# Hybrid decoder layer on one core: GpSimd's clears and copies moved or delayed, gate weights over its own queue, half of the value pages gathered, decay load and decay factors ahead

## The chip, the core and the metric

The kernel runs on one core of a Trainium2 chip. The metric is the device time of one execution in microseconds, the median of several runs; lower is better. The engines are named as in the profile: PE (TensorE), DVE (VectorE), ACT (ScalarE), POOL (GpSimd) and SP (SyncE, which here only issues transfers). POOL too issues transfers, plain ones and gathers by a list of row numbers.

## The reference

One step of a decoder layer for a prompt of 512 tokens and, beside it, 8 sample sequences of 4 new tokens each (544 token columns in all, model width 1024). The mixer has 8 attention heads of a native sparse attention (NSA: a compressed, a selected and a window branch, 2 key/value heads of 64) and 4 heads of gated linear attention (GLA: keys of 64, values of 128, chunks of 32 tokens). The parts that the change touches, in float32:

```python
def gla_branch(q_g, k_g, v_g, lr, w_gk, b_gk, s0):
    log_a = jax.nn.log_sigmoid((lr @ w_gk + b_gk)) / GLA_NORMALIZER
    o, S = gla_chunked(q_g, k_g, v_g, log_a.reshape(B, T, GLA_HEADS, GLA_DK), s0)
...
def mixer_output(o_cmp, o_slc, o_win, gates, o_gla, g_gla, gla_norm, w_o):
    o_nsa = gates[:, :, 0] * o_cmp + gates[:, :, 1] * o_slc + gates[:, :, 2] * o_win
    o_g = rmsnorm(o_gla, gla_norm) * jax.nn.silu(g_gla)
    return jnp.concatenate([o_nsa, o_g], axis=-1) @ w_o
...
past = cache_kv[page_table].reshape(B, past_len, 4, NSA_KV_HEADS, HEAD_DIM)
```

Here `lr` (16 columns), `g_gla` (512 columns), the queries, keys and values are all column groups of one projection of the normed input. Past keys and values of the samples lie in pages of 128 rows, 8 pages for each of the 8 sequences, in an order that a page table gives. After the mixer come a SwiGLU layer (inner width 2816), a gated per-layer embedding and a last norm.

## The kernel before, in words

Activations are kept feature by token: 8 slices of 128 features by 544 columns, in two halves of 256 and 288 columns. Every projection runs in three matmuls on split numbers: a value x is xh (rounded to the matmul's type) plus xl (the rest), a weight is `wh` plus `wl`, and `acc3` (L140) adds wh·xh, wh·xl and wl·xh. `fetch` (L115) loads 128 × 1024 weights (512 KB) over SP's queue into one of two `wraw` buffers; `load_w` (L122) makes `wh` from it, on ACT or (with `lo=POOL`) on POOL at L130, and `wl` by a subtraction, on DVE at L137 in one piece or on POOL at L135 in four pieces of 256 columns. `fm_tile` loads one such tile and runs its 2 × 24 matmuls into `pj`.

The instructions of each engine run in order. The order comes from a scheduler that goes by the order of the program, by data, and by hints: `issue_after` puts an instruction behind a given one, `together` (L46) draws a group of matmuls ahead and ties it to the loads that it needs.

The mixer goes through these places, with their times in the profiled execution:

- **Compression and queries, up to 136 us.** `compress_pages` gathers pages and compresses blocks of keys and values (`cps`); beside it `gates` (L515), the query tiles `q0` to `q3`, and behind the last compressed block `decays` (L534 to L561). It loads the small weight `wgk`, clears `w3` and `g3` (named `w` and `g` in the trace) on POOL, fills them with the split halves of `wgk` and of `glr` on ACT and DVE (L542 to L547), and multiplies them on PE (`zps`). The logarithm of the decay, `ls`, goes to memory (`lsd`) over POOL's queue.
- **Attention, 136 to 272 us**, prompt blocks and sample scores, with key pages loaded by SP beside it.
- **The GLA stretch, from 272 us.** The tile `gg0` of the GLA gate projection runs on PE. Small constants and `ls` are loaded (L997 to L1008). For the samples, `sps` sums the decays, ACT and DVE make `qs`, `ksm` and `kds`, POOL copies `qs` into `qm` (L1029), cleared before (L1016), and `oiq` multiplies `qm` by the old states. For the prompt, `gla_front` (L1048) makes `bps` and `rps`, and fills `kdz`, which POOL cleared (L1046). `gla_states`, `gla_out` and `gla_gate` follow.
- **The values of the samples, 278 to 373 us.** `s_values` (L943) is a generator: `tick` takes four steps of it behind each half of a gate tile. A step is one of 13 key tiles `kt` of a group `bg` of four sequences: tiles 0 to 7 are cache pages, 8 to 11 window rows, the last is new tokens. A page tile takes four pages into one of four `vch` buffers. One of its four pages is gathered by POOL (`gather_page`, L97), the other three are loaded by SP (`load_page`, L101), which first reads the page's number into a register.
- **Output projection, from about 375 us.** The first products (`pk`) of `wo` start while the last values and gate tiles end, and then the rest of the layer, up to 908 us.

The three hints that set the work around the change are:

```python
ready.append((load_page if b4 else gather_page)(vt[:, b4, :], m, i["pgv"]))
...
with tc.issue_after(pe[0].ins), together(ready, 5 * AHEAD):
...
def tile_gg(j, lo=POOL):
    fm_tile(f"gg{j}", ev_silu(j), lo=lo, then=tick)
```

Of the kernel before, what the change touches and what calls it, by code (L numbers as in the profile page):

```python
# [9 lines left out]
F32 = mybir.dt.float32  # L10
F32R = mybir.dt.float32r
# [10 lines left out]
TT = SEQ + NS  # L22
# [9 lines left out]
FM = FM_GLA + FM_NSA  # L32
# [3 lines left out]
def kernel(ctx: ExitStack, tc: tile.TileContext, i: dict, o: dict):  # L36
# [4 lines left out]
    def pool(name, bufs=1, space=None, stack=ctx, side=None):  # L41
        kw = {"reuse_waits": "tile"}
        if space is not None:
            kw["space"] = space
        if side is not None:
            kw["side"] = side  # L46
        return stack.enter_context(tc.tile_pool(name=name, bufs=bufs, **kw))
# [64 lines left out]

    third, count = [], [0, 0, 0]

    def fetch(src, n):  # L115
        own, b = (third[0], 1) if third and count[1] % 3 == 0 else (wp, 2)
        raw = own.tile([128, 1024], F32, name="wraw", bufs=b)
        count[1] += 1
        sp[0] = SP.dma_start(raw[:, :n], src)
        return raw  # L120

    def load_w(src, n, lo=None, dst=None, raw=None):  # L122
# [408 lines left out]
            DVE.tensor_copy(gate[bg], ps[:, 0:4])  # L531


    def decays(dp):  # L534

        wgk = dp.tile([64, 256], F32, name="wgk")
        SP.dma_start(wgk[32:49, :], i["wgk"])
        w3 = dp.tile([96, 256], F32R, name="w3")
        g3 = dp.tile([96, TT], F32R, name="g3")
        for t in (w3, g3):  # L540
            POOL.memset(t.bitcast(F32), 0.0)
        ACT.copy(w3[32:49, :], wgk[32:49, :])  # L542
        ACT.copy(w3[64:81, :], wgk[32:49, :])
        DVE.tensor_sub(w3[0:17, :], wgk[32:49, :], w3[32:49, :])
        ACT.copy(g3[32:49, :], glr[32:49, :])
        ACT.copy(g3[0:17, :], glr[32:49, :])
        DVE.tensor_sub(g3[64:81, :], glr[32:49, :], g3[32:49, :])  # L547
        ls = dp.tile([128, 5, 256], F32, name="ls")
        zm = dp.tile([128, 5, 256], F32, name="zm")
        POOL.memset(ls[:, 4, :], 0.0)  # L550
        POOL.memset(zm[:, 4, :], 0.0)
        for a, b, n in ((0, 2, 128), (2, 4, 128), (4, 5, 32)):
            ps = g1("zps").rearrange("p (t c) -> p t c", t=2)
            for t in range(a, b):
                mm(ps[:n, t - a, :], g3[:, 128 * t:128 * t + n], w3)
            ACT.activation(ls[:n, a:b, :], ps[:n, 0:b - a, :], AF.Abs)
            ACT.activation(zm[:n, a:b, :], ps[:n, 0:b - a, :], AF.Relu, scale=-1.0)
            ACT.activation(ls[:n, a:b, :], ls[:n, a:b, :], AF.Exp, scale=-1.0)
        ACT.activation(ls, ls, AF.Ln, bias=1.0)
        POOL.tensor_tensor(ls, zm, ls, op=ALU.add)  # L560
        POOL.dma_start(lsd, ls)  # L561
# [63 lines left out]
    later[3][1]()  # L625
    compress_prompt()
    gates()

    SP.dma_start(rowv, i["rowv"])
    rv = tp_.tile([128, 2496], F32, name="rv")  # L630
# [19 lines left out]
    first.close()  # L650
    y = compress_pages()
    with ExitStack() as dcy:
        decays(pool("dp", stack=dcy))
    fm_tile("q3", ev_q(3))
    second_layer(y)
    cpool.close()
# [274 lines left out]
    gp = pool("gp", stack=nsa)  # L931
# [11 lines left out]
    def s_values():  # L943
        for bg in range(2):
            P = SG[bg][0]
            O = psg.tile([128, 512], F32, name="sO", tag="sO", bufs=1)
            for kg_ in range(4):
                n = min(4, 13 - 4 * kg_)
                tp = proj_ps("sT")
                pT = sp_.tile([128, 512], F32, name="pT", bufs=2)  # L950
                for j in range(n):
                    kt = 4 * kg_ + j
                    w = 128 if kt < 12 else 72
                    PE.transpose(tp[0:w, 128 * j:128 * j + 128], P[:, 128 * kt:128 * kt + w], ident)
                if n == 4:
                    (ACT.copy if kg_ % 2 else DVE.tensor_copy)(pT, tp)
                else:
                    DVE.tensor_copy(pT[0:72, 0:128], tp[0:72, 0:128])
                for j in range(n):
                    kt = 4 * kg_ + j  # L960
                    w = 128
                    ready = []
                    if kt < 8:
                        vt = sp_.tile([128, 4, 128], F32, name="vch", bufs=4)
                        for b4 in range(4):
                            m = 8 * (4 * bg + b4) + kt
                            ready.append((load_page if b4 else gather_page)(vt[:, b4, :], m, i["pgv"]))
                    elif kt < 12:
                        vt = sp_.tile([128, 4, 128], F32, name="vch", bufs=4)
                        ready.append(SP.dma_start(vt, i["winv"][bg, kt - 8]))  # L970
                    else:
                        vt, w = VT[:, 4 * bg:4 * bg + 4, :], 72
                    with tc.issue_after(pe[0].ins), together(ready, 5 * AHEAD):
                        for b4 in range(4):
                            c = 128 * j + 32 * b4
                            mm(O[32 * b4:32 * b4 + 32, 0:128], pT[0:w, c:c + 32], vt[0:w, b4, :], start=kt == 0, stop=kt == 12)
                    yield
            Os = sp_.tile([128, 128], F32, name="Os", bufs=2)
            ACT.copy(Os, O[:, 0:128])
            tp = g1("sOT")  # L980
            PE.transpose(tp[:, 0:128], Os, ident)
            for g in range(2):
                DVE.tensor_copy(om_n[64 * g:64 * g + 64, :, SEQ + 16 * bg:SEQ + 16 * bg + 16].rearrange("p r (b t) -> p b r t", t=4),
                                tp[64 * g:64 * g + 64, 0:128].rearrange("p (b h r t) -> p b h r t", b=4, h=2, r=4)[:, :, g])
# [6 lines left out]
            next(values, None)  # L991

    def tile_gg(j, lo=POOL):
        fm_tile(f"gg{j}", ev_silu(j), lo=lo, then=tick)


    tri = gp.tile([128, 3, 128], F32, name="tri")  # L997
    SP.dma_start(tri, i["tri"])
    tri4 = gp.tile([32, 3, 32], F32, name="tri4")
# [4 lines left out]
    SP.dma_start(glan, i["glan"])  # L1004
    glah = gp.tile([128, 1], F32, name="glah")
    DVE.tensor_scalar_mul(glah, glan, 0.5)
    ls = gp.tile([128, 5, 256], F32, name="ls")
    SP.dma_start(ls, lsd)  # L1008


    qs = gp.tile([128, 2, NS], F32, name="qs")
# [1 line left out]
    ksm = gp.tile([128, 2, NS], F32, name="ksm")  # L1013
    kds = gp.tile([128, 2, NS], F32, name="kds")
    Es = gp.tile([128, 2, NS], F32, name="Es")
    POOL.memset(qm, 0.0)  # L1016
    for ip in range(2):
        cs = slice(ip * 128, ip * 128 + 128)
        sps = g1("sps")
# [6 lines left out]
        DVE.tensor_mul(qs[:, ip, :], qg[:, ip, SEQ:], Es[:, ip, :])  # L1026
        DVE.tensor_mul(ksm[:, ip, :], kg[:, ip, SEQ:], Ens[:, 0, :])
        DVE.tensor_mul(kds[:, ip, :], kg[:, ip, SEQ:], Ens[:, 1, :])
        POOL.tensor_copy(qm[:, ip, :].rearrange("p (b c) -> p b c", c=36)[:, :, 0:4],  # L1029
                         qs[:, ip, :].rearrange("p (b t) -> p b t", t=4))  # L1030
    atm = gp.tile([32, 4, 32], F32, name="atm")
    for hh in range(2):
# [10 lines left out]
    DVE.tensor_copy(kdT.rearrange("p a b -> p (a b)"), kdTp[0:32, 0:256])  # L1043

    kdz = gp.tile([128, 4, 4, 128], F32, name="kdz")
    POOL.memset(kdz, 0.0)  # L1046

    def gla_front(ip):  # L1048
        cs = slice(ip * 128, ip * 128 + 128)
# [13 lines left out]
        for t in range(4):  # L1063
            PE.transpose(kdp[:, t * 128:t * 128 + 128], X[:, t * 128:t * 128 + 128], ident)
        kv = kdp.rearrange("p (t c) -> p t c", t=4)
        for c in range(4):
            cp_ = slice(32 * c, 32 * c + 32)
            (ACT.copy if c % 2 else DVE.tensor_copy)(kdz[cp_, :, c, :], kv[cp_])
# [124 lines left out]
    states.append(gla_states(1, fronts[1][0]))  # L1193
    ogs = [og for ip in range(2) for og in gla_out(ip, *fronts[ip][1:3], states[ip])]
    for hd in (0, 1):
        tile_gg(hd)
    for hd in (0, 1):
        gla_gate(hd, ogs[hd])
    for hd in (2, 3):
# [391 lines left out]
```

## Time and profile before

| what | us |
|---|---|
| median of 3 runs (lowest, highest) | 914.95 (913.19, 914.98) |
| the profiled execution | 910.03 |
| its span, first to last instruction | 908.2 |
| PE busy in it | 861.9 (95%) |
| DVE busy | 500.4 (55%) |
| ACT busy | 352.9 (39%) |
| POOL busy | 150.9 (17%) |
| mean granted clock of PE | 0.977 of full speed |

The span is one execution as the hardware profiler took it. Busy time counts instructions at work; register and issuing instructions don't count. [...] In a timeline a row is a start, a duration, the engine, the line, the operation, what it writes and reads, how many alike were put together, and in brackets how long the engine idled before and what ended that.

### The profile page before, as it was taken

How to read it: one execution, taken by the hardware profiler on the slowest of the kernel's cores; microseconds unless marked ns; L12 is line 12 of the kernel's file. 1: busy time of each engine (PE TensorE's matmuls, PEld its weight loads, DVE VectorE, ACT ScalarE, POOL GpSimd, SP SyncE). 2: the span in 40 equal slices, each digit the busy share in tenths (PEclk: the TensorE clock that was granted, in tenths of full speed). 3: DMA queues.
4: the chain of work that ended last, by engine and by line, in shares of the span. 5: the costliest groups of instructions: out<-in, count | busy, mean ns of one | idle time of the engine just before them, and what ended most of it. 6: DMA issues, size and time to landing. Idle time of an engine off the chain costs nothing.

```text
span 908.2 us, 18054 instructions
## 1 busy us (share of the span) xinstructions
PE 861.9 (95%) x6872; PEld 797.3 (88%) x6872; DVE 500.4 (55%) x1223; ACT 352.9 (39%) x864; POOL 150.9 (17%) x182
## 2 busy tenths in 40 slices
PE   6999989999997998799999999999999999999995
PEld 6899978776566765799999999999999999999994
DVE  6635367777863654566455555555554243335654
ACT  7344376567653611434222333332323232224322
POOL 3544253000008223370000000000000000001511
PEclk9999999999998999899999999999999999999998
DMA  8676322332205233561133332332222222233111
GB/s 254 204 216 205 124 84 84 94 105 81 73 1 155 79 104 96 170 233 66 59 116 117 116 113 90 113 106 92 94 93 83 87 89 81 88 111 141 47 53 46
DMA packets 58821, 99.08 MB, mean 109 GB/s; under 512 B 11319, under 2 KB 40264, under 8 KB 58352
## 3 DMA queue, kind: packets, MB, share of 16 engines
q1 hardware_dynamic: 55296, 90.33, 30.6%
q0 software_dynamic: 2192, 5.90, 2.2%
q10 hardware_dynamic: 1248, 1.70, 0.5%
q8 instruction: 54, 0.88, 0.4%
q14 instruction: 31, 0.25, 0.1%
HBM read 91.74 MB, written 10.37 MB: 112 GB/s over the span
## 4 chain that ended last, share of the span: by engine, by line
PE 69%; issue 4%; POOL 3%; DVE 2%; DMA 2%; ACT 1%; SPq 1%; DVEq 0%; POOLq 0%; ACTq 0%
PE pg L57 17%; PE pu L57 15%; PE pd L57 14%; PE pj L57 5%; PE pk L57 4%; PE sc L57 3%; PE pO L57 2%; PE pT L769 2%; PE U L57 2%; DMA wraw<-in_wo 2%; POOL wl L135 1%; PE sS L57 1%; PE go L57 1%; PE sO L57 1%; PE oiq L57 1%
## 5 line engine op out<-in xcount | busy, mean ns | idle before, releaser
L132 ACT CAST wh<-wraw 128x1024 fp32r<-128x1024 f32 (+1 forms) x89 | 91.7, 1030 | 181.5 <-issue 78.5
L137 DVE TENSOR_TENSOR wl<-wraw,wh 128x1024 fp32r<-128x1024 f32 (+1 forms) x85 | 102.3, 1203 | 89.2 <-ACT wh L132 88.3
L57 PE MATMUL pg<-xh,wh 128*128 128x256 f32 (+1 forms) x400 | 115.7, 289 | 0.0
L57 PE MATMUL pg<-xl,wh 128*128 128x256 f32 (+1 forms) x400 | 115.2, 288 | 0.0
L57 PE MATMUL pg<-xh,wl 128*128 128x256 f32 (+1 forms) x400 | 114.6, 286 | 0.0
L57 PE MATMUL pd<-hh,wl 128*128 128x256 f32 (+1 forms) x352 | 101.8, 289 | 0.0
L57 PE MATMUL pd<-hl,wh 128*128 128x256 f32 (+1 forms) x352 | 101.6, 289 | 0.0
L57 PE MATMUL pd<-hh,wh 128*128 128x256 f32 (+1 forms) x352 | 101.6, 289 | 0.0
L57 PE MATMUL pu<-xh,wh 128*128 128x256 f32 (+1 forms) x352 | 101.5, 288 | 0.0
L57 PE MATMUL pu<-xl,wh 128*128 128x256 f32 (+1 forms) x352 | 101.3, 288 | 0.0
L57 PE MATMUL pu<-xh,wl 128*128 128x256 f32 (+1 forms) x352 | 100.8, 286 | 0.0
L57 PE MATMUL pj<-xh,wh 128*128 128x256 f32 (+1 forms) x272 | 83.1, 308 | 10.0 <-ACT wh L132 7.9
L57 PE MATMUL pj<-xl,wh 128*128 128x256 f32 (+1 forms) x272 | 81.4, 301 | 0.0
L176 POOL TENSOR_TENSOR prs<-pst,mhalf 128x2 f32<-128x2 f32 (+1 forms) x9 | 6.0, 672 | 452.4 <-DVE pst L175 452.4
L57 PE MATMUL pj<-xh,wl 128*128 128x256 f32 (+1 forms) x256 | 78.5, 306 | 1.6 <-POOL wl L135 1.6
L57 PEld LDWEIGHTS pg<-xh,wl 128*128 128x128 f32 x400 | 75.3, 188 | 0.0
L57 PEld LDWEIGHTS pg<-xl,wh 128*128 128x128 f32 x400 | 75.1, 188 | 0.0
L57 PEld LDWEIGHTS pg<-xh,wh 128*128 128x128 f32 x400 | 75.0, 188 | 0.1
L57 PEld LDWEIGHTS pd<-hh,wh 128*128 128x128 f32 x352 | 66.3, 188 | 0.1
L57 PEld LDWEIGHTS pu<-xh,wl 128*128 128x128 f32 x352 | 66.3, 188 | 0.0
L57 PEld LDWEIGHTS pd<-hl,wh 128*128 128x128 f32 x352 | 66.3, 188 | 0.0
L57 PEld LDWEIGHTS pd<-hh,wl 128*128 128x128 f32 x352 | 66.2, 188 | 0.0
(396 smaller groups left out, 2064.1 us busy)
## 6 DMA issues: line engine op xcount, KB each, us to landing
wraw<-in_wg SPq DMA_DIRECT2D x22, 512.0 KB
wraw<-in_wu SPq DMA_DIRECT2D x22, 512.0 KB
wraw<-in_win_fm SPq DMA_DIRECT2D x17, 512.0 KB
wraw<-in_wd SPq DMA_DIRECT2D x16, 512.0 KB
xc<-in_pgc SPq DMA_DIRECT2D x32, 128.0 KB
kch<-in_pgk SPq DMA_DIRECT2D x64, 64.0 KB
wraw<-in_wo SPq DMA_DIRECT2D x8, 512.0 KB
wraw<-in_wpg SPq DMA_DIRECT2D x8, 512.0 KB
```

Source lines behind the costliest of these rows:

```text
L57: pe[0] = PE.matmul(out, lhsT, rhs, start=start, stop=stop)
L132: ACT.copy(wh[:, :n], raw[:, :n])
L135: POOL.tensor_tensor(wl[:, c:c + 256], raw[:, c:c + 256], wh[:, c:c + 256], op=ALU.subtract)
L137: lo_[0] = DVE.tensor_sub(wl[:, :n], raw[:, :n], wh[:, :n])
L176: POOL.tensor_tensor(r[0:m, b:e], a[0:m, b:e], mhalf[0:m, b:e], op=ALU.pow)
L769: PE.transpose(tp[:, 128 * r:128 * r + 128], Ps[r][b][:, 128 * kt:128 * kt + 128], ident)
```

## The change

Six edits, in the order of the program:

1. `decays` is cut in two. `decay_factors` loads `wgk` and builds `w3` and `g3`, and is called right behind `gates`; `decays` keeps the product and what follows.
2. The load of `ls` is issued ahead of the other small loads of the GLA stretch.
3. `qm` is cleared on DVE instead of POOL, and `qs` is copied into it on ACT instead of POOL.
4. `kdz` is cleared in `gla_front(0)`, right before it is filled, and no longer ahead of it.
5. Of each four value pages two are gathered instead of one: 32 gathers and 32 loads by SP, where it was 16 and 48.
6. `gg0` is converted by ACT and DVE. The weights of `gg1` to `gg3`, which POOL converts as before, are loaded over POOL's queue.

```diff
-    def fetch(src, n):
+    def fetch(src, n, queue=SP):
...
-        sp[0] = SP.dma_start(raw[:, :n], src)
+        sp[0] = queue.dma_start(raw[:, :n], src)
...
-    def decays(dp):
-
-        wgk = dp.tile([64, 256], F32, name="wgk")
+    def decay_factors():
+
+        wgk = cp.tile([64, 256], F32, name="wgk")
         SP.dma_start(wgk[32:49, :], i["wgk"])
-        w3 = dp.tile([96, 256], F32R, name="w3")
-        g3 = dp.tile([96, TT], F32R, name="g3")
+        w3 = cp.tile([96, 256], F32R, name="w3")
+        g3 = cp.tile([96, TT], F32R, name="g3")
...
+        return w3, g3
+
+    def decays(dp, w3, g3):
...
     gates()
+    wg3 = decay_factors()
...
-        decays(pool("dp", stack=dcy))
+        decays(pool("dp", stack=dcy), *wg3)
...
-                            ready.append((load_page if b4 else gather_page)(vt[:, b4, :], m, i["pgv"]))
+                            ready.append((load_page if b4 % 2 else gather_page)(vt[:, b4, :], m, i["pgv"]))
...
     def tile_gg(j, lo=POOL):
-        fm_tile(f"gg{j}", ev_silu(j), lo=lo, then=tick)
+        w = load_w(None, 1024, lo, raw=fetch(i["win_fm"][FM.index(f"gg{j}")], 1024, POOL if lo else SP))
+        fm_tile(None, ev_silu(j), w, then=tick)
...
+    ls = gp.tile([128, 5, 256], F32, name="ls")
+    SP.dma_start(ls, lsd)
     tri = gp.tile([128, 3, 128], F32, name="tri")
...
-    ls = gp.tile([128, 5, 256], F32, name="ls")
-    SP.dma_start(ls, lsd)
...
-    POOL.memset(qm, 0.0)
+    DVE.memset(qm, 0.0)
...
-        POOL.tensor_copy(qm[:, ip, :].rearrange("p (b c) -> p b c", c=36)[:, :, 0:4],
+        ACT.copy(qm[:, ip, :].rearrange("p (b c) -> p b c", c=36)[:, :, 0:4],
...
-    POOL.memset(kdz, 0.0)
...
+        if ip == 0:
+            POOL.memset(kdz, 0.0)
...
-        tile_gg(hd)
+        tile_gg(hd, POOL if hd else None)
```

Where the order of the instructions changes, at three places.

POOL, from the end of attention on, before (`wl` and `wh` are the gate tiles' halves, the gathers fetch value pages):

```order
L130 TENSOR_SCALAR wh<-wraw 128x1024
L1016 MEMSET qm 128x576
L1046 MEMSET kdz 128x2048
L1142 MEMSET kd_4296 96x512
L98 DMA vch<-in_pgv,pidx 128x128 x4
L135 TENSOR_TENSOR wl<-wraw,wh 128x256 x4
L130 TENSOR_SCALAR wh<-wraw 128x1024
L135 TENSOR_TENSOR wl<-wraw,wh 128x256 x2
L1029 COPY qm<-qs 128x8x4
L135 TENSOR_TENSOR wl<-wraw,wh 128x256
L1029 COPY qm<-qs 128x8x4
```

The same place now:

```order
L119 DMA wraw<-in_win_fm 128x1024
L1071 MEMSET kdz 128x2048
L1148 MEMSET kd_4296 96x512
L98 DMA vch<-in_pgv,pidx 128x128 x8
L130 TENSOR_SCALAR wh<-wraw 128x1024 x2
L135 TENSOR_TENSOR wl<-wraw,wh 128x256 x8
L98 DMA vch<-in_pgv,pidx 128x128 x4
L119 DMA wraw<-in_win_fm 128x1024
L98 DMA vch<-in_pgv,pidx 128x128 x4
L1082 MEMSET S 128x128
```

The clear of `qm` and the copies into it have gone; eight gathers stand ahead of both conversions, and the third gate load stands between the gathers of the next pages.

PE at the decay product, before, inside the second half of `q3`:

```order
L57 MATMUL pj<-xh,wl 128x288
L57 MATMUL pj<-xh,wh 128x288
L57 MATMUL zps<-w_1661,g_1662 128x256 x4
L57 MATMUL pj<-xl,wh 128x288
L57 MATMUL pj<-xh,wl 128x288
```

And now, at the end of `q2`, whose last matmuls stand ahead of it, with `q3` (halves of 256 columns first) behind it:

```order
L57 MATMUL cps<-xc,w_182 128x128 x16
L57 MATMUL pj<-xh,wl 128x288
L57 MATMUL pj<-xh,wh 128x288
L57 MATMUL pj<-xl,wh 128x288
L57 MATMUL pj<-xh,wl 128x288
L57 MATMUL pj<-xh,wh 128x288
L57 MATMUL pj<-xl,wh 128x288
L57 MATMUL pj<-xh,wl 128x288
L57 MATMUL zps<-w_1521,g_1522 128x256 x4
L57 MATMUL pj<-xh,wh 128x256
```

The product has moved up by some thirty matmuls.

SP at the end of the sample's values, before:

```order
L104 DMA vch<-in_pgv 128x128
L970 DMA vch<-in_winv 128x512 x3
L119 DMA wraw<-in_win_fm 128x1024
L970 DMA vch<-in_winv 128x512
L119 DMA wraw<-in_wo 128x1024 x4
L78 DMA h<-in_xT 128x4x256 x2
```

And now, the start of the last series of pages, eight in all, and behind the last of them:

```order
L119 DMA wraw<-in_wo 128x1024 x2
L1120 DMA out_st_p<-S 64x128 x2
L104 ISA
L104 DMA vch<-in_pgv 128x128
L104 ISA
L104 DMA vch<-in_pgv 128x128
```

```order
L104 DMA vch<-in_pgv 128x128
L974 DMA vch<-in_winv 128x512 x4
L119 DMA wraw<-in_wo 128x1024 x2
L78 DMA h<-in_xT 128x4x256 x2
```

The gate weights (`in_win_fm`) have left SP's queue, two loads of the output weights have moved ahead of the last eight pages, and two have stayed behind them.

## Rows read from the trace of the kernel before

**Rows 1.** Slices: us, busy PE, PEld, DVE, ACT, POOL, PEclk, DMA share, GB/s.

```profile
113.50:136.20 22.70, 19.73 (x147) 18.00 (x145) 14.66 (x22) 15.91 (x36) 12.37 (x12) 0.92 0.23 83
136.20:272.40 136.20, 130.75 (x913) 96.55 (x914) 99.61 (x431) 87.34 (x322) 7.46 (x17) 0.97 0.24 73
272.40:295.10 22.70, 18.02 (x126) 15.22 (x127) 8.08 (x22) 7.61 (x25) 18.72 (x24) 0.81 0.50 155
363.20:385.90 22.70, 17.56 (x138) 15.96 (x135) 12.32 (x29) 9.14 (x22) 6.81 (x6) 0.81 0.50 171
476.70:499.40 22.70, 22.70 (x184) 22.70 (x183) 12.94 (x24) 6.87 (x12) 0.00 (x0) 1.00 0.35 117
```

**Rows 2.** PE's waits: us in total, times, longest; all of the span.

```profile
PE pj L57 <- ACT wh L132: 7.9, 1, 7.9
...
PE sO L57 <- DMA vch<-in_winv: 2.8, 2, 1.7
...
PE pj L57 <- POOL wh L130: 1.7, 1, 1.7
PE sO L57 <- DMA vch<-in_pgv: 1.7, 1, 1.7
```

**Rows 3.** Timeline of PE around the decay product: start, us, operation, idle before.

```profile
118.84 0.30 PE L57 MATMUL pj<-xh,wl 128*128 128x288 f32 x1
118.97 0.29 PE L57 MATMUL pj<-xh,wh 128*128 128x288 f32 x1
122.24 0.92 PE L57 MATMUL zps<-w,g 96*128 96x256 f32 x4 [2.97 <-DVE w L544]
122.96 0.44 PE L57 MATMUL pj<-xl,wh 128*128 128x288 f32 x1
...
125.36 0.44 PE L57 MATMUL pj<-xh,wl 128*128 128x288 f32 x1
```

**Rows 4.** Timeline of PE in the GLA stretch.

```profile
283.73 1.04 PE L57 MATMUL sps<-tri,ls 32*128 32x32 f32 x8 [0.78 <-DMA ls<-lsd]
...
286.90 0.58 PE L57 MATMUL pj<-xh,wl 128*128 128x256 f32 x1 [1.63 <-POOL wl L135]
...
291.65 0.42 PE L57 MATMUL oiq<-s,qm 64*32 64x128 f32 x2 [2.11 <-POOL qm L1029]
...
293.58 1.91 PE L57 MATMUL bps<-tri,ls 128*128 128x128 f32 x8
...
295.28 1.71 PE L57 MATMUL rps<-tri,ls 128*128 128x128 f32 x8
...
315.24 0.94 PE L57 MATMUL bps<-tri,ls 128*128 128x128 f32 x6
```

**Rows 5.** Timeline of POOL from the GLA stretch to the output weights.

```profile
274.25 2.81 POOL L135 TENSOR_TENSOR wl<-wraw,wh 128x256 fp32r<-128x256 f32 x4
...
278.59 1.80 POOL L1046 MEMSET kdz<- 128x2048 f32 x1
...
285.83 3.12 POOL L135 TENSOR_TENSOR wl<-wraw,wh 128x256 fp32r<-128x256 f32 x4
...
291.39 0.21 POOL L1029 COPY qm<-qs 128x32 f32<-128x32 f32 x1
...
366.27 1.04 POOL L130 TENSOR_SCALAR wh<-wraw 128x1024 fp32r<-128x1024 f32 x1 [10.79 <-DMA wraw<-in_win_fm]
...
382.92 6.07 POOL L135 TENSOR_TENSOR wl<-wraw,wh 128x256 fp32r<-128x256 f32 x4 [12.74 <-ACT wh L132]
```

**Rows 6.** Timeline of SP's queue, the last series of value pages.

```profile
339.14 19.91 SPq L104 DMA_DIRECT2D vch<-in_pgv  x18
```

**Rows 7.** View of tile vch: ns min/median/max, first and last start; then all its loads.

```profile
L98 POOL DMA_INDIRECT vch<-in_pgv,pidx x16: 940/950/1242, 281.0 to 353.4; - x16
...
DMA to landing us min/median/max: 2.4/2.8/6.2
```

**Rows 8.** Costliest groups on the page: busy us, mean ns; idle before.

```profile
L137 DVE TENSOR_TENSOR wl<-wraw,wh 128x1024 fp32r<-128x1024 f32 (+1 forms) x85 | 102.3, 1203 | 89.2 <-ACT wh L132 88.3
```

## The prediction

> **What bounds the kernel now.** First the engines, slice by slice: TensorE is busy nearly all the time, and in a typical slice of the second half, the last one of [rows 1], it has no gap and the full clock. [...] The largest single wait of all, 7.9 us on ACT's `wh`, lies at the start of the program; the change leaves it alone [rows 2].
>
> Second, what ended each gap: the decay projection `zps` waited 2.97 for a DVE subtraction [rows 3]; `sps` 0.78 for the load of `ls`, a projection 1.63 for POOL's `wl`, `oiq` 2.11 for POOL's copy into `qm` [rows 4]; the value product `sO` 1.7 for pages and 2.8 for window rows, and one projection 1.7 for POOL's `wh` [rows 2]. These are the waits that the change handles, 13.7 us together.
>
> Third, the late engine's own timeline. In the GLA stretch POOL converts gate weights, clears `kdz`, and issues four gathers of about 1.25 us each; the first `qm` copy stands behind all of that at 291.39 [rows 5]. In the last stretch SP issues 18 pages in 19.91 us [rows 6], and only behind them the last gate weights, for which POOL then waits 10.79 us, until 366.27 [rows 5].
>
> **The change part by part.** The sum is made on the profiled execution, 910.0 us, which lies 4.9 us under the median of the three runs, 914.95; I take the saving as the same for both.
>
> *Decays (113 to 136 us).* The factors depend on `glr` and on a small load alone, and are now built right behind the gates. What `zps` waited for was the last subtraction into `w`, and that stood behind compression work on DVE and ACT. The same operations now run some 40 us earlier, where TensorE has projections queued; they cost nothing as long as that queue lasts (uncovered, the six of ACT and DVE are bounded by the wait that they cause now, 2.97). `zps` itself moves up, ahead of `q3`. The load of `wgk` passes a dozen earlier transfers in SP's queue, one short issue there, and the store of the result on POOL's queue comes some 4 us sooner with `zps`, as do the loads behind it. Behind the old wait eleven projections come every 0.24 us where they came every 0.13 before it [rows 3], 1.2 us, and `zps` is stretched by some 0.2: 1.4 for the lower clock. The term is −4.4. Bounds: −5, if a little more of the slice's lower clock goes, and 0, if the attention stage behind takes it all.
>
> *GLA stretch (272 to 297 us).* Of the waits 0.78, 1.63 and 2.11 go [rows 4], 4.5 together: `ls` is issued ahead of four small loads, POOL no longer clears `qm` nor copies into it, and `gg0` is converted by ACT and DVE. The lower clock: `bps` and `rps` take 1.70 us from start to start, where six of the eight take 0.94 later at full clock [rows 4], so some 0.7 too much for each; and between 286.90 and 293.58, 6.7 us with 2.1 of wait, most of the work is stretched, by 1.6 if two thirds of it ran at half speed. That is 3.0, and 7.5 in all. Against it stand four new costs:
> - DVE makes `gg0`'s low part in one piece of 1.20 us [rows 8], where POOL's first quarter was ready after some 0.7 [rows 5]. Price 0.4, bounds 0 to 1.2.
> - `qm`'s clear on DVE (576 columns of `kdz`'s 2048 in 1.80, so some 0.5 at POOL's pace) and two copies on ACT at POOL's 0.21 [rows 5]: ahead of need, hence 0; 0.9 without cover.
> - `sps` now stands inside `gg0`'s second half with only four projections, 0.5 us, before the first matmul that needs what ACT and DVE make of it. Price 0.6, bounds 0 to 1.2.
> - POOL issues eight gathers before it touches `gg1`: 8 × 1.25 = 10 us, then two casts and the first quarters. From 281 that is about 294; by the new order TensorE comes to `gg1` only behind `bps`, `rps`, 32 `oiq` matmuls and three value products, at about the same time. Then POOL must finish `gg2` before it gathers the pages for `kt` 4 to 7. Price 1.5, bounds 0 to 6.
>
> The term is −7.5 + 2.5 = −5.0.
>
> *End of the values (356 to 386 us).* With half the pages gathered, SP's last series is 8 pages instead of 18, and 10 × 1.1 = 11 us shorter [rows 6]. `gg3` no longer stands behind it, as its load goes by POOL's queue, and two output weight loads are now ahead of the pages. So the waits 1.7, 2.8 and 1.7 go, 6.2 us. The slice's clock of 0.81 means (1 − 0.81) × 2 = 38% at the lower level, 8.6 us, of which 5.1 are idle; the 3.5 that were busy would take half, so 1.8 us come back. Given back: POOL issues 16 gathers more, 20 us of its time, out of the 10.79 and 12.74 that it idled before its last conversions [rows 5]; half of them stand among powers (`gst`) and conversions that wait for TensorE, and every gather waits for one of four `vch` buffers. I take 2.5, near the low end because the idle time covers nearly all of the 20; bounds 0 to 8. The term is −8.0 + 2.5 = −5.5.
>
> *Moved and free.* The clear of `kdz` (1.80 on POOL [rows 5]) still comes before the gathers in POOL's new order, ahead of anything late.
>
> [...] The rows first: a gather holds POOL 0.94 to 1.24 us, and a `vch` load lands 2.8 us after its issue, the median [rows 7]. [...]
>
> The sum: −4.4 − 5.0 − 5.5 = −14.9. The profiled execution would take 895.1, and the median 914.95 − 14.9 = **900.0 us**.
>
> **The rivals.**
> *POOL becomes the engine that is late, and the kernel gets slower.* POOL now carries 32 gathers and three gate tiles in one queue, in order. Its four subtractions took 2.81 and 3.12 us, but 6.07 at 382.92, while DVE subtracted too [rows 5]. If all of POOL's work doubles like that, the eight first gathers and `gg1`'s low part come 8 + 3 us later, less the 2 that they may have to spare: 9. The pages for `kt` 4 to 7 cost 6, the bound above. In the last series eight gathers stand among the `gst` powers, on which the gating of the last heads waits: 6 more. With 3.0 of lower clock around these waits, as now in the GLA stretch, that is 24, against 4.4 + 6.5 + 8.0 = 18.9 without POOL's costs: 5 slower, **920**. It decides from the point at which a gather holds POOL some 1.75 us on average instead of 0.98. Against it: all 16 gathers took 0.94 to 1.24 [rows 7]. [...] Chance 0.08.
>
> *The decays' gain is lost in attention.* If the stage from 136 to 272 us is paced by ACT and DVE, an earlier start ends in more waits there, and −4.4 becomes 0: 904.4. For it: DVE and ACT are busy 99.6 and 87.3 us of its 136 [rows 1]. Against it: TensorE is busy 130.8 and idles only 5.5. Chance 0.15.
>
> *Only SP's relief works.* New waits at `gg1` and at `kt` 4 to 7 take all of the GLA term and half of the last: 914.95 − 4.4 − 2.75 = 907.8. Chance 0.12.
>
> *The change only moves waits about.* The value products stay late, since `vch` still has four buffers; then the lower clock stays too, and some 1 us is won: 914, within the 0.2% (1.8 us) that a measurement of this kernel can tell from no change. Chance 0.05.
>
> *Nothing is given back.* All named waits and their lower clock go: 4.4 + 7.5 + 8.0 = 19.9, so 895.0. Chance 0.12.
>
> **How the numbers follow.** My forecast, 897 to 903, has 0.48. Faster: 0.48 + 0.15 + 0.12 + 0.12 = 0.87; same 0.05; slower 0.08. The range takes in the cases at 895.0, 904.4 and 907.8 with the bounds of their costs: 891 to 911. It leaves out "slower" and "same", 0.13, and a few hundredths of tails.
>
> **What would show it.** Right: `zps` without a wait and projections every 0.13 us behind it; no wait of `oiq` on POOL, and eight `bps` in about 1 us; granted clocks above 0.95 in the slices of [rows 1]; no projection that waits for `gg3`; SP's last series half as long. Wrong: waits of `sO` or of a projection on POOL's gathers or `wl` of over 3 us; gathers of over 1.5 us each; new short waits in attention that add up to 4 us.

## The result: slower, 930.59 us

The changed kernel takes 930.59 us (median of 4 executions, 927.26 to 931.74) against 914.97 for the kernel before (4 executions beside it, 913.19 to 917.10): a ratio of 1.0152, 95% interval 1.0121 to 1.0184. Forecast were 900.0 and a range of 891 to 911.

The page of the profile after, busy time and two lines of its 40 slices:

```profile
PE 867.1 (94%) x6872; PEld 800.1 (86%) x6872; DVE 506.6 (55%) x1225; ACT 354.4 (38%) x867; POOL 163.8 (18%) x193
...
PE   5898999999897889899999999999999999999994
...
PEclk9999999999999978899999999999999999999997
```

POOL is busy 18% of the span and bounds nothing by its own work. The low clock is still there: in the slices from 324 to 393 us (7, 8 and 8 tenths granted) instead of those near 285 and 375.

The waits of PE after the change, from the view of waits (us in total, times, longest):

```profile
PE pj L57 <- issue: 4.5, 6, 1.0
PE kdTp L1047 <- DVE atm L1042: 4.1, 1, 4.1
PE cps L57 <- DMA xc<-in_pgc: 3.6, 1, 3.6
PE U L57 <- DVE kdz L1074: 3.0, 1, 3.0
...
PE zps L57 <- ACT zm L560: 1.2, 1, 1.2
```

All waits that the prediction wanted to remove are gone: `zps` for DVE, `sps` for `ls`, `oiq` for POOL's `qm` [rows 3, 4], `sO` for pages and window rows, the projection for the last `wh` [rows 2]. New ones stand in their place, and none of them is put down to POOL (but "issue" says only that no releaser is on record). SP's queue and the view of the tile `vch` (ns min/median/max, first and last start):

```profile
364.27 11.09 SPq L104 DMA_DIRECT2D vch<-in_pgv  x8
```

```profile
L98 POOL DMA_INDIRECT vch<-in_pgv,pidx x32: 940/952/1070, 283.7 to 378.9; - x32
```

SP's last series is 8 pages, as forecast (18 before [rows 6]), but it starts 25 us later. A gather holds POOL as long as before, 952 ns against 950 (medians) [rows 7].

Where the time went is best read by stages. Their ends are the first and last starts of the tiles `cps`, `sc`, `sps`, `go` and `pk` in the tile view (us; behind the comma the chip of the trace; "first" is that of the result, whose number isn't known and may be one of the others; nor is the chip of the trace shown ahead of the prediction):

| trace, chip | first cps | to sc | attention | to sps | GLA | to pk | rest | span |
|---|---|---|---|---|---|---|---|---|
| before [rows 1], not known | 45.5 | 90.5 | 130.0 | 17.7 | 65.4 | 29.3 | 529.8 | 908.2 |
| changed, first | 47.3 | 91.9 | 131.8 | 16.6 | **78.2** | 27.9 | 531.8 | 925.5 |
| before (e11), 0 | 45.6 | 90.5 | 130.2 | 17.5 | 63.7 | 30.3 | 530.7 | 908.5 |
| changed (e8), 0 | 45.4 | 86.5 | 138.3 | 16.7 | 61.8 | 23.4 | 531.5 | 903.6 |
| decays alone (e3), 8 | 45.8 | 86.1 | 131.6 | 17.6 | 64.1 | 30.0 | 530.4 | 905.6 |
| 32 gathers alone (e4), 8 | 45.8 | 90.6 | 130.1 | 17.5 | 69.0 | 23.9 | 532.7 | 909.6 |
| 32 gathers alone (e14), 6 | 46.4 | 94.1 | 130.1 | 17.5 | **85.5** | 25.8 | 531.7 | 931.1 |
| gates by SP (e9), 0 | 45.9 | 86.2 | 131.3 | 17.5 | 63.1 | 24.4 | 531.6 | 900.0 |
| gates by SP (e13), 6 | 46.5 | 87.7 | 130.1 | 19.2 | **78.0** | 27.5 | 531.9 | 920.9 |
| 16 gathers, gates by SP (e15), 6 | 48.1 | 91.8 | 134.4 | 18.1 | 62.6 | 31.1 | 530.7 | 916.8 |
| gates alone (e6), 12 | 45.9 | 91.7 | 130.6 | 19.8 | 63.1 | 20.4 | 531.7 | 903.2 |
| gates alone (e18), 5 | 45.5 | 90.5 | 130.6 | 19.9 | 63.1 | 20.1 | 532.1 | 901.8 |
| no value gathers (e17), 5 | 46.0 | 90.9 | 130.0 | 17.5 | 67.0 | **48.2** | 529.9 | 929.5 |

The trace of e15 is that of its longest execution (918.54; the other eight took 907.55 to 911.55).

On the chip of the result the GLA stretch is 12.8 us longer than before. On chip 0 the same kernel is not slower at all. So the first thing that the experiments found was the chip.

**What is late.** The timeline of the changed kernel on the chip of the result, in three places (start, us, operation, idle before and its releaser):

```profile
290.64 0.25 PE L57 MATMUL attps<-qs,ksm 64*32 64x32 f32 x4
...
291.19 0.27 PE L958 MATMUL sT<-c_ident,Ps 128*128 128x128 f32 x1
...
292.60 0.94 POOL L98 DMA_INDIRECT vch<-in_pgv,pidx  x1 [0.30 <-issue]
...
295.28 0.34 DVE L1042 TENSOR_TENSOR atm<-attps,tri 32x64 f32<-32x64 f32 x2 [5.52 <-remote]
...
295.54 0.61 PE L1047 MATMUL kdTp<-c_ident,kds 128*32 128x128 f32 x2 [4.08 <-DVE atm L1042]
...
331.06 0.29 PE L57 MATMUL pj<-xh,wl 128*128 128x288 f32 x1
...
333.62 0.95 POOL L98 DMA_INDIRECT vch<-in_pgv,pidx  x1 [0.30 <-issue]
...
335.93 0.46 DVE L941 TENSOR_TENSOR om_g<-pj,rb 128x288 f32<-128x288 f32 x1 [3.77 <-remote]
...
337.03 0.69 PE L57 MATMUL U<-vg,kdz 128*64 128x128 f32 x4 [3.01 <-DVE kdz L1074]
...
365.76 0.27 PE L57 MATMUL go<-S,qe 64*32 64x128 f32 x1
...
371.65 0.28 PE L57 MATMUL pj<-xh,wl 128*128 128x256 f32 x1 [0.94 <-issue]
...
373.13 0.60 ACT L1125 ACTIVATE og<-go 128x512 f32<-128x512 f32 x1 [14.46 <-remote]
```

The same operations on chip 0 (e8):

```profile
289.86 0.25 PE L57 MATMUL attps<-qs,ksm 64*32 64x32 f32 x4
...
290.14 0.34 DVE L1042 TENSOR_TENSOR atm<-attps,tri 32x64 f32<-32x64 f32 x2 [1.17 <-PE attps L57]
...
324.94 0.29 PE L57 MATMUL pj<-xh,wl 128*128 128x288 f32 x1
...
325.27 0.46 DVE L941 TENSOR_TENSOR om_g<-pj,rb 128x288 f32<-128x288 f32 x1 [0.66 <-PE pj L57]
...
348.70 0.27 PE L57 MATMUL go<-S,qe 64*32 64x128 f32 x1
...
349.07 0.60 ACT L1125 ACTIVATE og<-go 128x512 f32<-128x512 f32 x1 [7.46 <-PE U L57]
```

On chip 0 DVE and ACT read a result of PE 0.28, 0.33 and 0.37 us after the matmul's start; on the chip of the result 4.64, 4.87 and 7.37 us after. On both chips POOL meanwhile issues gathers: the last of eight in a row at the first two places, six in a row at the third ("remote" stands where the releaser has no record). Five matmuls that start between 290.31 and 291.06 have their signals recorded together at 295.21 to 295.36, and what waits for them stands. At the third place PE itself stands too, three times for 0.9 to 1.0 us without a releaser on record; the stretch to `pk` is 4.5 us longer than on chip 0. Between the start of a `go` matmul and ACT's `og` at this place lie 6.5 to 7.4 us in all six traces with 32 gathers on the late chips (the first, 12 and 6), and 0.4 in the four on chips 8 and 0. In the compression stage, with gathers four in a row, the same shows on a smaller scale: near 70 us ACT waits for `cps` until 2.6 us after the matmul's start in all eight traces of the late chips, with 16 value gathers too, and in none of the other twelve.

**What it costs.** About half is idle time, the other half work at the lower clock. Busy time and granted clock in windows of the changed kernel on the chip of the result, the whole GLA stretch first (us, PE, PEld, DVE, ACT, POOL, PEclk, DMA share, GB/s; PEclk is the granted share of full speed, and windows within one level read 0.50 or 1.00):

```profile
287.60:365.80 78.20, 66.16 (x663) 47.52 (x662) 36.59 (x96) 22.77 (x69) 37.79 (x43) 0.87 0.26 83
...
295.00:298.00 3.00, 2.46 (x12) 2.40 (x13) 1.37 (x5) 0.59 (x3) 2.60 (x4) 0.53 0.00 0
298.00:301.00 3.00, 3.00 (x39) 2.48 (x38) 2.48 (x3) 2.68 (x9) 3.00 (x4) 0.90 0.00 0
...
331.00:337.00 6.00, 2.07 (x15) 1.50 (x13) 1.76 (x4) 0.87 (x2) 3.90 (x4) 0.93 0.30 77
337.00:352.00 15.00, 14.97 (x105) 9.86 (x105) 5.72 (x14) 1.42 (x3) 2.97 (x5) 0.50 0.22 80
355.00:358.00 3.00, 3.00 (x41) 1.72 (x41) 1.60 (x4) 0.00 (x0) 0.00 (x0) 1.00 0.06 14
```

and on chip 0 (e8), where this work comes a little earlier:

```profile
286.90:348.70 61.80, 58.36 (x660) 43.02 (x662) 38.31 (x96) 22.45 (x69) 38.18 (x43) 0.97 0.34 105
...
330.00:345.00 15.00, 14.76 (x181) 10.09 (x180) 10.30 (x28) 1.26 (x3) 4.46 (x6) 1.00 0.23 80
```

PE idles 3.9 us of six, and then works 15 us without a gap at the level of 0.50. At the full level, 1.00, that work would take half, an estimate from the two levels: 7.5 us. With the 3.9 before it and the 4.1 at `kdTp` this is 15.5 of the 16.4 by which the GLA stretch is longer than on chip 0. The whole stretch says the same: PE idles 12.0 us instead of 3.4, 8.6 more, and is busy 66.2 instead of 58.4, 7.8 more.

### The profile page after: what moved, and what is told of

It is laid out like the page before. It is cut to its first block, busy times and chain, and to the rows that moved or that the text cites. A ratio compares the mean times of both kernels' runs of the same rounds, so it can differ in the third digit from the quotient of the medians.

```text
span 925.5 us, 17979 instructions
## 1 busy us (share of the span) xinstructions
PE 867.1 (94%) x6872; PEld 800.1 (86%) x6872; DVE 506.6 (55%) x1225; ACT 354.4 (38%) x867; POOL 163.8 (18%) x193
## 4 chain that ended last, share of the span: by engine, by line
PE 78%; DVE 6%; issue 5%; DMA 3%; ACT 3%; POOL 2%; SPq 1%; another core or an unknown queue 1%; DVEq 0%; ACTq 0%; POOLq 0%
PE pg L57 16%; PE pu L57 14%; PE pd L57 14%; PE pj L57 9%; PE pk L57 5%; PE cps L57 3%; PE pO L57 3%; PE U L57 2%; PE pT L773 2%; PE sc L57 2%; PE sO L57 1%; PE go L57 1%; DMA xc<-in_pgc 1%; PE sS L57 1%
## 5 line engine op out<-in xcount | busy, mean ns | idle before, releaser
L137 DVE TENSOR_TENSOR wl<-wraw,wh 128x1024 fp32r<-128x1024 f32 (+1 forms) x86 | 103.1, 1199 | 90.6 <-ACT wh L132 89.1
L57 PEld LDWEIGHTS pd<-hh,wl 128*128 128x128 f32 x352 | 66.2, 188 | 0.0
```

The costliest lines, as they stand in the source:

```text
L57: pe[0] = PE.matmul(out, lhsT, rhs, start=start, stop=stop)
L137: lo_[0] = DVE.tensor_sub(wl[:, :n], raw[:, :n], wh[:, :n])
```

## The experiments

My theory after the result was that the 16 added gathers on POOL cost the time; the rivals were that the gate loads in POOL's queue do, that the decays do, and, once the single parts cost nothing, that the chip decides. The kernels of one group ran on one chip: e1 to e4 on chip 8 (before 910.02), e5 to e7 on 12 (912.44), e8 to e11 on 0 (910.39), e12 to e15 on 6 (913.64), e16 to e18 on 5 (911.18). Some expectations name theories by letters: D is that gathers and gate loads on POOL's queue cost only together, F that the chip decides, G that on a chip that loses the 16 added gathers alone do it.

**e1: the added gathers undone.** Changed kernel with a quarter of the pages gathered, as before.

```
-  ready.append((load_page if b4 % 2 else gather_page)(vt[:, b4, :], m, i["pgv"]))
+  ready.append((load_page if b4 else gather_page)(vt[:, b4, :], m, i["pgv"]))
```

> The changed kernel with one edit taken back: 16 value pages gathered and 48 loaded by SP, as before the change; the other five edits stay. Theory A (the 16 added gathers on POOL's queue cost the time; while they run, TensorE's results reach the other engines late): the stretch from the first sO to the last one becomes about 13 us shorter than in the changed kernel, and the time is 915 or less, ratio to the kernel before 0.99 to 1.00. Theory B (the early decay factors and the order of SP's queue in the compression stage cost it): no more than 3 us come back, ratio 1.012 to 1.016. Theory C (gate weights over POOL's queue): as B.

Measured: 905.7, ratio 0.9954 [0.9931, 0.9977].

**e2: gate weights back on SP's queue**, the 32 gathers kept.

```
-  w = load_w(None, 1024, lo, raw=fetch(i["win_fm"][FM.index(f"gg{j}")], 1024, POOL if lo else SP))
+  w = load_w(None, 1024, lo, raw=fetch(i["win_fm"][FM.index(f"gg{j}")], 1024, SP))
```

> The changed kernel with the gate weights gg1 to gg3 loaded over SP's queue again; gg0 stays with ACT and DVE, all else as changed. Theory C (three loads of 512 KB through POOL's queue cost the time): ratio to the kernel before about 1.000 to 1.005. Theories A and B: ratio 1.010 to 1.020, since gg3 may come behind SP's pages again.

Measured: 902.3, 0.9917 [0.9888, 0.9945].

**e3: decays alone.** Kernel before with `decay_factors` split off and called behind `gates()`, nothing else.

```
-    def decays(dp):
+    def decay_factors():
...
+    wg3 = decay_factors()
...
-        decays(pool("dp", stack=dcy))
+        decays(pool("dp", stack=dcy), *wg3)
```

> The kernel before with the split of the decays alone: factors built right behind the gates. Theory B (this part delays the compression stage by 5.5 us, since SP's transfers there come later, and wins 4.3 back at zps): ratio 1.000 to 1.010, the last cps matmuls of the value group 5 us later than before. Theory A (this part does what the prediction says, and the late compression stage of the changed kernel has another cause): ratio 0.995, cps as early as before and zps without its wait of 3 us.

Measured: 907.88, 0.9987 [0.9963, 1.0011].

**e4: the gathers alone.** Kernel before with the one line of e1 the other way round:

```
-  ready.append((load_page if b4 else gather_page)(vt[:, b4, :], m, i["pgv"]))
+  ready.append((load_page if b4 % 2 else gather_page)(vt[:, b4, :], m, i["pgv"]))
```

> The kernel before with the split of the value pages alone: 32 gathered, 32 loaded by SP. Theory A: ratio 1.010 to 1.016, the loss between 290 and 370 us, with waits of 3 to 5 us for a TensorE result while gathers are issued. Theories B and C: ratio 0.994 to 1.000, since SP's last series of pages is shorter and nothing else moves.

Measured: 910.21, 1.0001 [0.9985, 1.0018]. Of e1 to e4 none is slower than the kernel before beyond its interval, so no part that was tried loses on this chip; e2 and e3 came out in neither theory's range, and theory A's for e4 (1.010 to 1.016) was missed. Either the loss needs several parts together, or the chip is another. Hence the next group.

**e5: the changed kernel again; e6: the gate part alone** (kernel before, `gg1` to `gg3` loaded by POOL's queue, `gg0` converted by ACT and DVE); **e7: the changed kernel without its decay part** (the edit of e3 taken back).

```
-  def fetch(src, n):
+  def fetch(src, n, queue=SP):
...
-  sp[0] = SP.dma_start(raw[:, :n], src)
+  sp[0] = queue.dma_start(raw[:, :n], src)
...
-  fm_tile(f"gg{j}", ev_silu(j), lo=lo, then=tick)
+  w = load_w(None, 1024, lo, raw=fetch(i["win_fm"][FM.index(f"gg{j}")], 1024, POOL if lo else SP))
+  fm_tile(None, ev_silu(j), w, then=tick)
...
-  tile_gg(hd)
+  tile_gg(hd, POOL if hd else None)
```

> The changed kernel once more, unaltered, beside the others on one chip. Theory D (32 gathers and three loads together on POOL's queue are what costs, neither alone): ratio to the kernel before 1.012 to 1.018 again, and in the trace TensorE's results reach the other engines 4 us late in places where POOL issues gathers, in the compression stage too. Theory E (the first comparison was of a disturbed chip): ratio 0.990 to 0.997, first cps of the value group at 97 to 98 us as in the kernel before, no late results.

> The kernel before with edit 6 alone: gg0 by ACT and DVE, gg1 to gg3 loaded over POOL's queue; 16 gathers as before. Theory D: ratio 0.995 to 1.005, no loss in the compression stage. Theory C (loads over POOL's queue cost by themselves): ratio above 1.008. Theory E: ratio 0.993 to 0.999.

> The changed kernel with the decay part taken back, 32 gathers and POOL's three loads kept. Theory D: ratio 1.010 to 1.018, as slow as the changed kernel or slower by its 4 us. Theory B (the early decay factors disturb the compression stage): ratio 0.990 to 1.000. Theory E: 0.997 to 1.002, some 4 us over the changed kernel of the same call.

Measured on chip 12: e5 930.47, 1.0183 [1.0113, 1.0253]; e6 905.52, 0.9906 [0.9879, 0.9933]; e7 929.94, 1.0183 [1.0125, 1.0241]. The loss is there again, the decays have no share in it, and the gate part alone gains 7 us, more than any theory expected.

**e8: the changed kernel a third time; e9 and e10: e2 and e1 again; e11: the kernel before, traced**, all on chip 0.

> The changed kernel a third time, now beside the two versions that each take back one edit, and beside the kernel before, all on one chip. Theory D (32 gathers and three loads together on POOL's queue cost about 25 us, on any chip): ratio to the kernel before 1.014 to 1.022. [...]

> The version with the gate weights on SP's queue, on this chip. Theory D: ratio 0.990 to 0.995, as on the first chip, whatever the changed kernel does beside it. Theory F: as slow as the changed kernel beside it, within 0.5%, since it has the same 32 gathers.

> The version with 16 gathers, on this chip. Theory D: ratio 0.993 to 0.998, as on the first chip. Theory F: between 0.995 and 1.010, if this chip is of the kind that loses, since the 16 gathers of before remain; else 0.993 to 0.998.

> The kernel before, unaltered, for its trace on this chip. Theory D: no late results of TensorE in its compression stage, first cps of the value group at 97.3 us as in the first trace. Theory F, on a chip of the kind that loses: late results of 1 to 4 us while the 32 gathers of the compression stage are issued, and the value group 1 to 6 us later than 97.3; ratio 1.000 in both.

Measured: e8 905.37, 0.9949 [0.9928, 0.9969]; e9 903.0, 0.9917 [0.9895, 0.9940]; e10 907.47, 0.9973 [0.9956, 0.9990]; e11 1.0000 [0.9987, 1.0013]. The kernel that was 1.5 and 1.8% slower in the first two comparisons is 0.5% faster here. e1 and e10 hold edit 6 together with edits 1 to 4 and 16 gathers; their 0.9954 and 0.9973 lie behind the 0.9906 of edit 6 alone (e6, another chip). So edits 1 to 4 add nothing to it in these runs; 2, 3 and 4 were never run alone.

**e12: the changed kernel a fourth time; e13: e2 a third time; e14: e4 again; e15: the changed kernel with both the edits of e1 and of e2**, so with 16 gathers and the gate weights on SP's queue.

> The changed kernel a fourth time, to tell of which kind this chip is. On a chip that loses: ratio 1.014 to 1.020 and late results of TensorE of 4 us or more between 280 and 380 us. On the other kind: 0.993 to 0.997 and none.

> 32 gathers, gate weights on SP's queue. On a chip that loses: theory D (gathers and POOL's weight loads together are needed for the loss) expects 0.990 to 0.996; theory G (the 16 added gathers alone bring it) 1.008 to 1.020. On the other kind both expect 0.990 to 0.994.

> The kernel before with 32 gathers alone. On a chip that loses: theory D expects 0.998 to 1.004; theory G 1.008 to 1.025. On the other kind both expect 0.998 to 1.002.

> The changed kernel with both POOL parts taken back: 16 gathers, gate weights on SP's queue; decays, order of the loads, clears and gg0 stay changed. It should win on chips of either kind: theory D and G both expect 0.990 to 0.997 and no late results of TensorE after 280 us.

Measured on chip 6: e12 929.45, 1.0186 [1.0139, 1.0234]; e13 923.11, 1.0084 [1.0051, 1.0118]; e14 931.33, 1.0185 [1.0147, 1.0223]; e15 911.01, 0.9960 [0.9938, 0.9982]. This group settles which part loses. e14 is the kernel of e4: the 16 added gathers and nothing else make 1.0001 on chip 8 and 1.0185 on chip 6, the whole loss, without any gate load on POOL's queue; so D falls. Without them the rest gains (e15), and with them it loses (e13): 911.01 against 923.11, so that within the changed kernel, gates by SP, the added gathers cost some 12 us on chip 6. e14 is not the gathers of the changed kernel alone, though: its PE waits 6.9 us at 296 us ("issue"), which is the wait that e4 lists as 6.7 us for POOL's `wl` of `gg1` behind the eight gathers, and which the changed kernel hasn't. As e4 has it too, it is not what parts the chips. Windows of e14, and then of e4 for the same stretch:

```profile
337.00:364.00 27.00, 25.24 (x173) 16.66 (x173) 9.46 (x24) 2.61 (x5) 5.83 (x7) 0.50 0.20 67
```

```profile
330.00:345.00 15.00, 15.00 (x180) 10.55 (x179) 8.75 (x23) 2.39 (x5) 7.17 (x9) 1.00 0.30 103
345.00:360.00 15.00, 12.36 (x165) 8.64 (x164) 7.00 (x16) 1.67 (x3) 8.27 (x9) 1.00 0.33 103
```

27 us at the lower level with PE 25.24 busy are some 12 of the 16.5 by which the GLA stretch differs.

**e16: the added pages as plain loads from POOL's queue.** Kernel before; of the 32 pages of e4, 16 go as gathers and 16 as direct loads that POOL issues with the index in a register.

```
+  def pool_page(dst, n, src):
+      v = POOL.value_load(pt[0:1, n:n + 1], min_val=0, max_val=src.shape[0] - 1)
+      return POOL.dma_start(dst, src[bass.ds(v, 1)].rearrange("a p c -> p (a c)"))
...
-  ready.append((load_page if b4 else gather_page)(vt[:, b4, :], m, i["pgv"]))
+  ready.append((load_page if b4 % 2 else gather_page if b4 == 0 else pool_page)(vt[:, b4, :], m, i["pgv"]))
```

> Kernel of before; of the 32 value pages that the change gathers, the 16 added ones are issued by POOL as direct loads (index read into a register, as SP does it), so POOL issues as many transfers at the same places as in the run with 32 gathers, but 16 of them without a table of addresses. If it is the gathers as such that make TensorE's results arrive late on the one kind of chip: there the time stays within 0.4% of before (ratio 0.996 to 1.004) and no result of TensorE after 280 us comes over 3 us late in the places of the added pages. If any transfer that POOL issues does it: about 1.018 on that kind of chip. On the other kind both expect 0.997 to 1.004.

**e17: no value page gathered**, all 64 by SP.

```
-  ready.append((load_page if b4 else gather_page)(vt[:, b4, :], m, i["pgv"]))
+  ready.append(load_page(vt[:, b4, :], m, i["pgv"]))
```

> Kernel of before with none of its 16 value pages gathered; all 64 go by SP. If the cost per gather is a steady one on the losing kind of chip (some 18 us for 16), it would gain there: down to 0.985, less what SP's longer series gives back (16 pages of 1.1 us, half of it uncovered, 9 us): 0.99 to 1.00. If a few gathers cost nothing and only the dense ones (8 in a row) do, it loses by SP's series alone: 1.00 to 1.01 on either kind.

**e18: the gate part alone, again.**

> Kernel of before with the gate weights of gg1 to gg3 on POOL's queue and gg0 converted by ACT and DVE, nothing else. It gave 0.9906 on a chip of the losing kind. If its gain is that of SP's last series and of gg3 being early, it holds on either kind: 0.989 to 0.994. If it was the lucky side of that kind of chip, 0.997 to 1.003 here.

Measured on chip 5: e16 908.66, 0.9968 [0.9947, 0.9989]; e17 931.29, 1.0217 [1.0176, 1.0258]; e18 901.99, 0.9897 [0.9877, 0.9917].

Chip 5 showed no late results in any of the three traces, not even in the compression stage, so e16 does not tell a gather from another transfer of POOL; that stays open. No kernel with eight gathers in a row ran on this chip. e16 shows another thing. Its eleven executions fall apart into eight of 904.7 to 908.7 and three of 914.8 to 918.9, and the traced one is of the three:

```profile
325.00:328.00 3.00, 2.02 (x19) 1.19 (x17) 2.75 (x8) 1.04 (x2) 2.47 (x3) 1.00 0.43 118
331.00:355.00 24.00, 24.00 (x162) 16.09 (x162) 9.43 (x24) 1.19 (x2) 5.46 (x7) 0.50 0.22 75
```

One microsecond of idle time, no late result, and then 24 us without a gap at the lower level: the GLA stretch takes 77.5 us here. So a large part of the loss can come without late results. In all six traces of late chips with 32 gathers such a stretch of 13.7 to 30.7 us begins between 335 and 342 us; in e2, e4, e8 and e9, 32 gathers on chips 8 and 0, there is none. But e1 (16 gathers, chip 8) has one of 13.7 us at 341, so late results are not all that it can follow. That the gap ahead of it brings it is argued from the order of events; no run put a gap there on purpose.

e17 was a miss for both theories, which had 0.985 to 1.01. Its waits of PE, its window near the end and SP's last series:

```profile
PE sO L57 <- DMA vch<-in_pgv: 19.4, 5, 4.3
```

```profile
360.00:400.00 40.00, 16.28 (x151) 11.58 (x149) 6.40 (x12) 4.25 (x9) 3.83 (x5) 0.66 0.35 112
```

```profile
344.12 36.94 SPq L104 DMA_DIRECT2D vch<-in_pgv  x32
```

32 pages in 36.94 us stand against 18 in 19.91 [rows 6]; the difference, 17.0, is nearly all of the 17.9 by which the stretch to `pk` grows against e11. A page on SP's queue costs its full 1.15 us there. The 16 gathers of the kernel before are worth some 18 us. The 16 that the change adds are worth 6.4 in this stretch by themselves (e4 against e11), and nothing once the gate loads have left SP's queue (23.4 in e8, 20.1 in e18 without them).

e18 tells where the gain of the change is. The last gate weights are converted early, on POOL's timeline:

```profile
318.53 1.05 POOL L130 TENSOR_SCALAR wh<-wraw 128x1024 fp32r<-128x1024 f32 x1 [5.61 <-PE pj L57]
```

Before it was at 366.27, behind a wait of 10.79 for the load [rows 5]. The stretch to `pk` is 10.2 us shorter than in e11, with 16 gathers. It is the loads that do it, not the conversion of `gg0`: e15, with `gg0` by ACT and DVE but all gate loads by SP, keeps 31.1 (in its longest execution). This one part alone (0.9906 on chip 12, 0.9897 on chip 5) is ahead of both kernels on either kind of chip, and has the lowest ratio of all versions; on chips 8 and 0 the changed kernel with its gate loads by SP (0.9917 twice) can't be told from it.

**What stays open.** Why the first chip, 12 and 6 deliver results late while POOL issues gathers, and 8, 0 and 5 don't. The traces differ in one more thing: those of the late chips hold 7,870 to 8,507 records of signals (the changed kernel, e5 to e7, e12 to e15), those of the others 9,457 to 9,583, and the missing ones lie in the same stretches: the changed kernel's trace has 731 from 280 to 360 us, where that of [rows 1] has 1,560, and 954 from 20 to 100 us, where that one has 1,857. No run shows whether the lateness and the missing records have one cause. Every execution timed here was recorded (each has a granted clock), so that the lateness belongs to recording and not to the kernel can't be ruled out, and a kernel without recording wasn't tried.

## Why the prediction was wrong, step by step

| term | forecast | chip 0, e8 less e11 | chip of the result |
|---|---|---|---|
| decays (start of `sc`) | −4.4 | −4.2 | +3.2 |
| attention | 0 | +8.1 | +1.8 |
| GLA (from `sc` to `go`) | −5.0 | −2.7 | +11.7 |
| end of the values (to `pk`) | −5.5 | −6.9 | −1.4 |
| rest | 0 | +0.8 | +2.0 |
| sum | −14.9 | −4.9 | +17.3 |

The last column sets the changed kernel's trace against the one of [rows 1], which has no late results; the medians of the result are 15.6 apart.

**The step that failed** is the price of the gathers: "POOL issues 16 gathers more, 20 us of its time, out of the 10.79 and 12.74 that it idled", 2.5, with a bound of 8. It counted what a gather takes from POOL, and that was right: 940 to 1070 ns, POOL 18% busy. It did not count what the rest of the core does meanwhile: on the late chips results of PE reach DVE and ACT 4.6 to 7.4 us after the matmul's start, and a long stretch at the lower clock follows. On chip 6 the added gathers cost some 12 us in the changed kernel (e13 against e15) and some 17 by themselves (e14, 1.0185), against a bound of 8 here and 6 in the GLA stretch. Where no results are late they cost nothing: on chip 0 e8 is 2.1 us faster than e10, which has 16 gathers.

**The rival that ends slower** had 920 and 0.08; the sign was its, the mechanism was not. It "decides from the point at which a gather holds POOL some 1.75 us"; the gathers held it 0.95. POOL's conversions did not double either: the four subtractions at 337.08 took 2.97, as the 2.81 and 3.12 before [rows 5]. The sentence that was to show the prediction wrong, waits on POOL's gathers or `wl`, names the wrong releaser; the waits of 4.1 and 3.0 are for DVE, which waited for PE. Waits of over 3 us for POOL's `wl` did come, in e4 (6.7) and e9 (3.1), two kernels that are not slower than the one before.

**The lower clock was priced only as something to win back.** The prediction took 3.0 and 1.8 for it where a wait went, and 3.0 in the rival. It counted work at the lower level as twice as long, from clock rates that no run shows; what the traces show is the levels, 0.50 and 1.00, and projections every 0.24 us instead of 0.13 [rows 3] at a granted clock of 0.50 (122.7 to 125.9 us). A new wait just ahead of the second half of the GLA stretch costs much more: 15 us at the lower level behind a gap of 3.9, so 7.5.

**The decays.** −4.2, and −4.5 in e3 against e4, at the start of `sc`, as forecast; the 2.97 of `zps` [rows 3] became 1.2, for ACT. But attention gives part of it back, the outcome of the rival to which 0.15 was given: in the nine traces of kernels with the old place of the decays it takes 130.0 to 131.6, on average 130.4, in the eleven with the new one 130.1 to 138.3, on average 133.3. The decays alone are worth 1.2 us by the ratio (e3, 0.9987, with an interval that holds no change) and 2.1 by the medians. The 8.1 of e8 is the most in any trace, and not by the rival's waits for ACT and DVE: PE idles 1.1 us more there than in e11, and is busy 130.48 us instead of 123.44, at a granted clock of 0.95 instead of 0.99. Why was not tested.

**The GLA stretch.** The waits named went, and in e8 the window from 285 to 300 us has PE busy 13.54 instead of 11.35 (e11). But of the 3.0 for the lower clock nothing came back: PE is busy 58.36 us of the whole stretch in e8 and 58.46 in e11, and the eight `bps` still take 1.71 from start to start (1.70 before). The eight gathers ahead of `gg1` cost no wait for POOL in e8; without the other edits (e4) they make the stretch 5.3 longer, near the bound of 6. −2.7 remained of −5.0.

**The end of the values.** −6.9 on chip 0 and −5.9 in e9, near the −5.5. The cause was only half right: e4 gets −6.4 from the gathers, and e18 −10.2 from the gate loads without them. The two reliefs don't add up, since both remove the same lateness. Whether the gate loads land later from POOL's queue than the other loads of `win_fm` from SP's the runs don't settle: 3.6 us after the issue against 3.3 in e18, 4.6 against 5.1 in e8 (medians). That they stand behind no pages there is worth 10.2 us (e18).

**The trace read.** The profiled execution of before took 910.0, like the kernel on chips 8, 0 and 5; the executions beside the result took 913 to 917, like those on chips 12 and 6. The prediction took "the saving as the same for both". That difference of 5 us was the one sign of it, and was passed over; the trace itself has no late result.

## What to carry to other kernels

Price a transfer that you add not only by what it holds its issuing engine, but by a trace on more than one chip with that transfer alone; the same edit was worth 0.0 and +1.9%. Look for stretches in which a gap ahead of much small work is followed by the lower clock and so costs a multiple of itself (3.9 us of idle time, then 15 us at 0.50 in the changed kernel; 1.0, then 24 in e16), and keep new waits out of them. Where two edits remove the same lateness, run each alone: here the smaller one, three gate loads moved to another queue (with `gg0` converted by ACT and DVE), had all of the gain.

## What the runs showed of the hardware

- On the first chip, 12 and 6 results of PE reached DVE and ACT late while POOL issued gathers: 4.6 to 7.4 us after the matmul's start at the three places shown, where it was 0.3 to 0.4 on chip 0, and PE itself paused for 0.9 to 1.0 us; with 16 value gathers (e6, e15) the GLA stretch took 63.1 and 62.6 us on the late chips too, as elsewhere.
- The lower clock lasted for at least 15 to 27 us while PE had no gap or small ones (14.97 of 15, 24.00 of 24, 25.24 of 27 us busy), behind idle times of 1 to 4 us. But in the same stretch of e4 PE idled 1.0 us in all from 325 to 331 us, and the clock stayed at 1.00.
- One kernel on one chip (e16) has two groups of times, some 10 us apart; the one trace, of the longer group, has the long stretch at the lower clock.
